# One image pair per DMA, with stores issued two pairs late, in a rotation kernel

## The chip, the cores and the metric

The kernel runs on one core of one Trainium2 chip. The metric is the device time of one execution in microseconds (us); the time quoted for a kernel is the median of several executions. A profile is a hardware trace of one further execution. In it PE is the matrix engine, ACT the scalar engine, DVE the vector engine, POOL the GpSimd engine, and SP the engine that issues the loads. "SPq" and "ACTq" are those engines' instruction queues where they issue DMAs.

## The reference

The input `x` has 32 x 3 = 96 images of 256 x 256 float32 values (25.17 MB), and so has the output. Each image is turned by 90 degrees:

```
batch, c, h, w = 32, 3, 256, 256
return np.rot90(x, k=1, axes=(-2, -1)).astype(np.float32)
```

No arithmetic is done on the values: 25.17 MB are read, moved to other places and 25.17 MB are written.

## The kernel before, in words

The 96 images are taken as 48 pairs. In SBUF a pair fills all 128 partitions: 64 partitions for each image, each holding four neighbouring rows (4 KB, one contiguous piece of DRAM). The pairs are grouped: eleven groups of four pairs (8 images, 2 MB), one of two pairs (1 MB) and two of one pair (512 KB each).

A group is loaded by one DMA on the SP queue (line 68) into a tile `S4` of `in_pool`, which has four buffers. Then each pair of the group goes through four steps:

- PE transposes it in eight pieces of 128x128 float32 into PSUM, tile `p1pair` (line 88);
- ACT casts each image's half to bf16 in two copies, tiles `bt` (line 96);
- PE multiplies by two exchange matrices, which reverse the order of rows, in four products into PSUM, tile `psum2` (line 102);
- DVE copies the result in two copies into the group's output tile `U4` (line 111).

When all the pairs of a group are done, one DMA on the ACT queue stores the group (line 118). `out_pool` has three buffers of 2 MB. The last three groups have tiles of their own (`tail_pool`), and their stores are issued after all compute (line 125).

PE, ACT and DVE each take their instructions in the order that the tile framework's scheduler writes; it puts transposes of the next pair between the products of the current one. The framework also adds the waits: a load waits until the transposes that read its buffer are done, a copy into `U4` waits until the store that read that buffer has landed, a store waits for its copies. DMAs get one of eight completion semaphores (`DMAHW0` to `DMAHW7`) in turn, loads and stores together in scheduled order, and a DMA is not issued before the previous DMA on its semaphore has landed. Instructions behind a waiting DMA on the same engine wait too.

In the trace the tile `S4` appears as `S_91`, `S_175` and so on, one name for each group, and `U4` as `U_93`, `U_177`, ..., `U_tail_1083`.

Of the kernel before, what the change touches and what calls it, by code (L numbers as in the profile page):

```python
# [1 line left out]

# [5 lines left out]


@with_exitstack
def kernel(
    ctx: ExitStack,
    tc: tile.TileContext,
    x: bass.AP,
    out: bass.AP,
):
    nc = tc.nc
    B, C, H, W = x.shape
    assert H == W == 256  # L20
    P = 128
    N = B * C

    x_v4 = x.rearrange("b c (p d) w -> (b c) p d w", d=4)
    out_v4 = out.rearrange("b c (p d) w -> (b c) p d w", d=4)

    GROUPS = [8] * 11 + [4, 2, 2]
    assert sum(GROUPS) == N
    assert all(g % 2 == 0 for g in GROUPS)

    fp32 = mybir.dt.float32
    bf16 = mybir.dt.bfloat16

    const_pool = ctx.enter_context(tc.tile_pool(name="const", bufs=1))
    in_pool = ctx.enter_context(tc.tile_pool(name="in_pool", bufs=4))
    bt_pool = ctx.enter_context(tc.tile_pool(name="bt_pool", bufs=4))
    out_pool = ctx.enter_context(tc.tile_pool(name="out_pool", bufs=3))
    tail_pool = ctx.enter_context(tc.tile_pool(name="tail", bufs=1))
    psum1_pool = ctx.enter_context(tc.tile_pool(name="psum1", bufs=2, space=bass.MemoryType.PSUM))
    psum2_pool = ctx.enter_context(tc.tile_pool(name="psum2", bufs=2, space=bass.MemoryType.PSUM))  # L40

    identity = const_pool.tile([P, P], fp32)
    make_identity(nc, identity)

    exchh = []
    for hh in range(2):
        e = const_pool.tile([P, P // 2], bf16, name=f"exch{hh}")
        nc.gpsimd.memset(e, 0.0)
        nc.gpsimd.affine_select(
            out=e,  # L50
            in_=e,
            compare_op=mybir.AluOpType.not_equal,
            fill=1.0,
            base=-(P - 1) + hh,
            pattern=[[2, P // 2]],
            channel_multiplier=1,
        )
        exchh.append(e)

    TAIL_N = 3  # L60
    deferred_stores = []

    i0 = 0
    for gi, G in enumerate(GROUPS):
        is_tail = gi >= len(GROUPS) - TAIL_N
        G2 = G // 2
        S4 = in_pool.tile([P, G2, 4, W], fp32, tag="S", name="S4")
        nc.sync.dma_start(
            out=S4[:],
            in_=x_v4[i0 : i0 + G].rearrange("(j q) p d w -> (q p) j d w", q=2),  # L70
        )
        S4_r = S4.rearrange("pp j d (k par) -> pp j d k par", par=2)

        if is_tail:
            U4 = tail_pool.tile(
                [P, G2, 4, W], fp32, tag=f"tail{gi}", name=f"U4_tail{gi}"
            )
        else:
            U4 = out_pool.tile([P, G2, 4, W], fp32, tag="U", name="U4")

        for j in range(G2):
            p1pair = psum1_pool.tile([P, 2, 2, W], fp32, name="p1pair")
            p1pair_r = p1pair.rearrange(
                "k dd q (pt dquad) -> k dd q pt dquad", dquad=4
            )
            for d4 in range(4):
                for par in range(2):
                    nc.tensor.transpose(  # L88
                        p1pair_r[:, 1 - par, :, :, d4],
                        S4_r[:, j, d4, :, par],  # L90
                        identity,
                    )
            bts = []
            for q in range(2):
                bt = bt_pool.tile([P, 2, W], bf16, name="bt")
                nc.scalar.copy(out=bt[:], in_=p1pair[:, :, q, :])  # L96
                bts.append(bt)

            psum2 = psum2_pool.tile([P, 2, 2, W], fp32, name="psum2")
            for hh in range(2):  # L100
                for q in range(2):
                    nc.tensor.matmul(  # L102
                        out=psum2[64 * q : 64 * q + 64, hh],
                        lhsT=exchh[hh][:],
                        rhs=bts[q][:],
                        start=True,
                        stop=True,
                    )

            for hh in range(2):  # L110
                nc.vector.tensor_copy(  # L111
                    out=U4[:, j, 2 * hh : 2 * hh + 2, :], in_=psum2[:, hh]
                )

        if is_tail:
            deferred_stores.append((i0, G, U4))
        else:
            nc.scalar.dma_start(
                out=out_v4[i0 : i0 + G].rearrange("(j q) p d w -> (q p) j d w", q=2),
                in_=U4[:],  # L120
            )
        i0 += G

    for s0, G, U4 in deferred_stores:
        nc.scalar.dma_start(
            out=out_v4[s0 : s0 + G].rearrange("(j q) p d w -> (q p) j d w", q=2),
            in_=U4[:],
        )


# [1 line left out]
_INS = ['x']  # L132
_OUTS = [((32, 3, 256, 256), 'float32')]


# [23 lines left out]
```

## Time and profile before

| | |
|---|---|
| median of 6 runs | 128.02 us (127.48 to 128.65) |
| profiled execution | 128.3 us, of which the span from the first to the last instruction is 126.5 us |
| PE busy | 103.4 us (82%), 576 matmuls |
| DVE busy | 60.6 us (48%), 96 copies |
| ACT busy | 51.9 us (41%), 96 casts and a table load |
| DMA | 50.42 MB in 12742 packets, mean 398 GB/s |
| DMAs issued by the kernel | 14 loads on SP, 14 stores on ACT |

"Busy" for an engine is the time in which it runs instructions; DMA issues are not counted. The DMA share is the mean busy share of the core's 16 DMA engines and can read slightly over 1, as packets overlap. "To landing" is the time from a DMA's issue to its completion semaphore. q1 is the queue of the loads and q10 that of the stores; both run on the same 16 DMA engines.

### The profile page before, as it was taken

Reading aid. Unit: us, or ns where it says so; the run is one execution under the profiler, and the core shown is the slowest. Engines: PE = TensorE matmul, PEld = TensorE weight load, DVE = VectorE, ACT = ScalarE, POOL = GpSimd, SP = SyncE. Lnnn points to the kernel's source line nnn. Section 1 sums busy time; section 2 is a strip of 40 time slices with the busy share of each in tenths; the row PEclk is TensorE's granted clock in tenths of the full one; section 3 lists DMA queues with packets and bytes.
Section 4 is the critical chain, followed back from the end, with each engine's and each line's share of the span. In section 5 each row is a group of like instructions: output and inputs, shape, how many; then the busy total and the mean of one; then the engine's idle time right before and its main releaser. Section 6 shows DMA issues by size and latency. Waiting matters only on the chain.

```text
span 126.5 us, 1521 instructions
## 1 busy us (share of the span) xinstructions
PE 103.4 (82%) x576; PEld 64.1 (51%) x576; DVE 60.6 (48%) x96; ACT 51.9 (41%) x97; POOL 1.2 (1%) x10
## 2 busy tenths in 40 slices
PE   0019999999999999999995995799999599999600
PEld 0018366565576566655752753476555456655300
DVE  0000447484566646745643741904940954746530
ACT  4003353445633563456336336053465065436300
POOL 3000000000000000000000000000000000000000
PEclk9999999999999999999999999689999999999965
DMA  3999999999999999999999999999999999999993
GB/s 85 399 370 409 417 416 409 412 378 413 426 418 423 421 418 425 414 417 425 418 421 426 417 425 416 418 414 427 416 421 426 416 416 426 414 376 394 405 411 140
DMA packets 12742, 50.42 MB, mean 398 GB/s; under 512 B 448, under 2 KB 448, under 8 KB 12736
## 3 DMA queue, kind: packets, MB, share of 16 engines
q1 hardware_dynamic: 6368, 25.17, 49.7%
q10 hardware_dynamic: 6368, 25.17, 48.7%
q8 instruction: 4, 0.07, 0.2%
q14 instruction: 2, 0.02, 0.0%
HBM read 25.17 MB, written 25.17 MB: 398 GB/s over the span
## 4 chain that ended last, share of the span: by engine, by line
DMA 41%; PE 40%; DVE 7%; ACT 6%; issue 1%; DVEq 1%; ACTq 0%
PE p1pair L88 25%; DMA out_dram<-U_597 18%; DMA out_dram<-U_345 16%; DMA S_91<-in_x_dram 6%; ACT bt L96 6%; DVE U_597 L111 2%; DVE U_849 L111 1%; DVE U_345 L111 1%; DVE U_tail_1017 L111 1%; DVE U_tail_1060 L111 1%; PE psum_127 L102 1%; PE psum_107 L102 1%; PE psum_419 L102 1%; PE psum_671 L102 1%; PE psum_1007 L102 1%
## 5 line engine op out<-in xcount | busy, mean ns | idle before, releaser
L96 ACT CAST bt<-p1pair 128x512 bf16<-128x512 f32 x96 | 50.6, 593 | 66.7 <-PE p1pair L88 66.7
L102 PEld LDWEIGHTS <-exch_81 128*64 128x64 bf16 x96 | 8.6, 108 | 19.2 <-issue 3.9
L88 PE MATMUL p1pair<-identity,S_91 128*128 128x128 f32 x32 | 6.9, 374 | 9.0 <-DMA S_91<-in_x_dram 9.0
L88 PEld LDWEIGHTS p1pair<-identity,S_91 128*128 128x128 f32 x32 | 5.5, 216 | 10.9 <-issue 10.9
L102 PEld LDWEIGHTS <-exch_86 128*64 128x64 bf16 x96 | 6.0, 110 | 5.1 <-issue 5.0
L111 DVE COPY U_93<-psum_107 128x512 f32<-128x512 f32 x2 | 1.3, 686 | 13.7 <-PE psum_107 L102 13.7
L88 PE MATMUL p1pair<-identity,S_679 128*128 128x128 f32 x32 | 6.1, 332 | 0.0
L88 PEld LDWEIGHTS p1pair<-identity,S_679 128*128 128x128 f32 x32 | 4.8, 212 | 2.1 <-issue 1.7
L88 PE MATMUL p1pair<-identity,S_175 128*128 128x128 f32 x32 | 5.7, 306 | 0.0
L88 PE MATMUL p1pair<-identity,S_763 128*128 128x128 f32 x32 | 5.6, 310 | 0.0
L88 PEld LDWEIGHTS p1pair<-identity,S_175 128*128 128x128 f32 x32 | 4.4, 208 | 2.4 <-issue 1.6
L88 PEld LDWEIGHTS p1pair<-identity,S_763 128*128 128x128 f32 x32 | 4.6, 210 | 1.7 <-issue 1.3
L88 PE MATMUL p1pair<-identity,S_847 128*128 128x128 f32 x32 | 5.3, 300 | 0.0
L88 PE MATMUL p1pair<-identity,S_343 128*128 128x128 f32 x32 | 5.3, 299 | 0.0
L88 PE MATMUL p1pair<-identity,S_931 128*128 128x128 f32 x32 | 5.3, 299 | 0.0
L88 PE MATMUL p1pair<-identity,S_427 128*128 128x128 f32 x32 | 5.3, 299 | 0.0
L88 PE MATMUL p1pair<-identity,S_595 128*128 128x128 f32 x32 | 5.3, 299 | 0.0
L88 PE MATMUL p1pair<-identity,S_511 128*128 128x128 f32 x32 | 5.3, 299 | 0.0
L88 PE MATMUL p1pair<-identity,S_259 128*128 128x128 f32 x32 | 5.3, 299 | 0.0
L88 PEld LDWEIGHTS p1pair<-identity,S_847 128*128 128x128 f32 x32 | 4.3, 209 | 1.7 <-issue 1.3
L88 PEld LDWEIGHTS p1pair<-identity,S_595 128*128 128x128 f32 x32 | 4.3, 208 | 1.7 <-issue 1.3
L88 PEld LDWEIGHTS p1pair<-identity,S_343 128*128 128x128 f32 x32 | 4.3, 208 | 1.7 <-issue 1.3
(164 smaller groups left out, 154.8 us busy)
## 6 DMA issues: line engine op xcount, KB each, us to landing
S_91<-in_x_dram SPq DMA_DIRECT2D x1, 2048.0 KB, 8.2
S_175<-in_x_dram SPq DMA_DIRECT2D x1, 2048.0 KB, 13.4
S_259<-in_x_dram SPq DMA_DIRECT2D x1, 2048.0 KB, 17.9
S_343<-in_x_dram SPq DMA_DIRECT2D x1, 2048.0 KB, 22.5
S_427<-in_x_dram SPq DMA_DIRECT2D x1, 2048.0 KB, 15.3
out_dram<-U_93 ACTq DMA_DIRECT2D x1, 2048.0 KB, 15.6
S_511<-in_x_dram SPq DMA_DIRECT2D x1, 2048.0 KB, 15.6
out_dram<-U_177 ACTq DMA_DIRECT2D x1, 2048.0 KB, 17.0
```

The costliest lines, as they stand in the source:

```text
L88: nc.tensor.transpose(p1pair_r[:, 1 - par, :, :, d4], S4_r[:, j, d4, :, par], identity,)
L96: nc.scalar.copy(out=bt[:], in_=p1pair[:, :, q, :])
L102: nc.tensor.matmul(out=psum2[64 * q : 64 * q + 64, hh], lhsT=exchh[hh][:], rhs=bts[q][:], start=True, stop=True,)
L111: nc.vector.tensor_copy(out=U4[:, j, 2 * hh : 2 * hh + 2, :], in_=psum2[:, hh])
```

## The change

Groups are given up. Each of the 48 pairs has its own 512 KB load, its own output tile and its own 512 KB store. `in_pool` has eight buffers of 512 KB (4 MB; before, four of 2 MB) and `out_pool` ten of 512 KB (5 MB; before, three of 2 MB, and 2 MB of tail tiles). The store of a pair is not issued right after its copies, but two pairs later, on the ACT queue between that later pair's transposes and its casts; after the last pair the remaining two are issued. The compute of a pair is the same.

```
-    GROUPS = [8] * 11 + [4, 2, 2]
-    in_pool = ctx.enter_context(tc.tile_pool(name="in_pool", bufs=4))
+    in_pool = ctx.enter_context(tc.tile_pool(name="in_pool", bufs=8))
-    out_pool = ctx.enter_context(tc.tile_pool(name="out_pool", bufs=3))
-    tail_pool = ctx.enter_context(tc.tile_pool(name="tail", bufs=1))
+    out_pool = ctx.enter_context(tc.tile_pool(name="out_pool", bufs=10))
...
+    STORE_LAG = 2
+    pending = []
+    def flush_store():
+        s0, U4s = pending.pop(0)
+        nc.scalar.dma_start(
+            out=out_v4[s0 : s0 + 2].rearrange("q p d w -> (q p) d w"),
+            in_=U4s[:],
+        )
+    for pi in range(NPAIR):
+        i0 = 2 * pi
+        S4 = in_pool.tile([P, 4, W], fp32, tag="S", name="S4")
         nc.sync.dma_start(
             out=S4[:],
-            in_=x_v4[i0 : i0 + G].rearrange("(j q) p d w -> (q p) j d w", q=2),
+            in_=x_v4[i0 : i0 + 2].rearrange("q p d w -> (q p) d w"),
         )
...
+        U4 = out_pool.tile([P, 4, W], fp32, tag="U", name="U4")
...
+        if len(pending) >= STORE_LAG:
+            flush_store()
...
+        pending.append((i0, U4))
-        if is_tail:
-            deferred_stores.append((i0, G, U4))
-        else:
-            nc.scalar.dma_start(
-                out=out_v4[i0 : i0 + G].rearrange("(j q) p d w -> (q p) j d w", q=2),
-                in_=U4[:],
-            )
-    for s0, G, U4 in deferred_stores:
-        nc.scalar.dma_start(...)
+    while pending:
+        flush_store()
```

In the built program of the changed kernel the order on the engines is this. PE runs the eight transposes of pair i+1 and then the four products of pair i, pair after pair. ACT runs the store of pair i-2 and then the two casts of pair i. The first eight loads take the semaphores 0 to 7; after a mixed stretch the loads settle on the semaphores 0, 2, 4 and 6 and the stores on 1, 3, 5 and 7. After the last load the remaining stores (pairs 38 to 47) take all eight in turn.

More of the change, by code (lines that the diff above doesn't have):

```diff
@@ L22 @@
     N = B * C
+    NPAIR = N // 2
     x_v4 = x.rearrange("b c (p d) w -> (b c) p d w", d=4)
     out_v4 = out.rearrange("b c (p d) w -> (b c) p d w", d=4)
-    GROUPS = [8] * 11 + [4, 2, 2]
-    assert sum(GROUPS) == N
-    assert all(g % 2 == 0 for g in GROUPS)
     fp32 = mybir.dt.float32
@@ L58 @@
         exchh.append(e)
[L60 to L67, printed above, removed]
+    STORE_LAG = 2
[9 more added lines that the diff above has]
+        S4 = in_pool.tile([P, 4, W], fp32, tag="S", name="S4")
@@ L68 @@
         nc.sync.dma_start(
             out=S4[:],
-            in_=x_v4[i0 : i0 + G].rearrange("(j q) p d w -> (q p) j d w", q=2),
+            in_=x_v4[i0 : i0 + 2].rearrange("q p d w -> (q p) d w"),
         )
-        S4_r = S4.rearrange("pp j d (k par) -> pp j d k par", par=2)
-        if is_tail:
-            U4 = tail_pool.tile(
-                [P, G2, 4, W], fp32, tag=f"tail{gi}", name=f"U4_tail{gi}"
-            )
-        else:
-            U4 = out_pool.tile([P, G2, 4, W], fp32, tag="U", name="U4")
@@ L81 @@
[L81 to L84, printed above, removed]
-            )
[L86 to L113, printed above, removed]
@@ L115 @@
-        if is_tail:
-            deferred_stores.append((i0, G, U4))
-        else:
-            nc.scalar.dma_start(
-                out=out_v4[i0 : i0 + G].rearrange("(j q) p d w -> (q p) j d w", q=2),
-                in_=U4[:],
-            )
-        i0 += G
-    for s0, G, U4 in deferred_stores:
[L125 to L128, printed above, removed]
+        S4_r = S4.rearrange("pp d (k par) -> pp d k par", par=2)
@@ new lines @@
+        U4 = out_pool.tile([P, 4, W], fp32, tag="U", name="U4")
+        p1pair = psum1_pool.tile([P, 2, 2, W], fp32, name="p1pair")
+        p1pair_r = p1pair.rearrange("k dd q (pt dquad) -> k dd q pt dquad", dquad=4)
+        for d4 in range(4):
+            for par in range(2):
+                nc.tensor.transpose(
+                    p1pair_r[:, 1 - par, :, :, d4],
+                    S4_r[:, d4, :, par],
+                    identity,
+                )
+        if len(pending) >= STORE_LAG:
+            flush_store()
@@ new lines @@
+        bts = []
+        for q in range(2):
+            bt = bt_pool.tile([P, 2, W], bf16, name="bt")
+            nc.scalar.copy(out=bt[:], in_=p1pair[:, :, q, :])
+            bts.append(bt)
+        psum2 = psum2_pool.tile([P, 2, 2, W], fp32, name="psum2")
+        for hh in range(2):
+            for q in range(2):
+                nc.tensor.matmul(
+                    out=psum2[64 * q : 64 * q + 64, hh],
+                    lhsT=exchh[hh][:],
+                    rhs=bts[q][:],
+                    start=True,
+                    stop=True,
+                )
@@ L132 @@
+        for hh in range(2):
+            nc.vector.tensor_copy(
+                out=U4[:, 2 * hh : 2 * hh + 2, :], in_=psum2[:, hh]
+            )
+        pending.append((i0, U4))
+    while pending:
+        flush_store()
 _INS = ['x']
```

## The prediction

> **What bounds the kernel now.** I read first the page's busy shares beside its DMA rows, then the load queue's waits and issue times, then the transfers by window, and last the time line of the end.
>
> ```profile
> span 126.5 us, 1521 instructions
> PE 103.4 (82%) x576; PEld 64.1 (51%) x576; DVE 60.6 (48%) x96; ACT 51.9 (41%) x97; POOL 1.2 (1%) x10
> DMA  3999999999999999999999999999999999999993
> ...
> HBM read 25.17 MB, written 25.17 MB: 398 GB/s over the span
> ```
>
> No engine is full, and the DMA engines are, in every slice but the first and the last.
>
> ```profile
> 4.00:24.00 20.00, 14.94 (x73) 9.56 (x73) 5.90 (x10) 6.44 (x12) 0.00 (x0) 1.00 1.02 405
> 24.00:28.00 4.00, 3.71 (x23) 2.28 (x23) 3.06 (x5) 1.12 (x3) 0.00 (x0) 1.00 1.02 383
> 28.00:68.00 40.00, 39.44 (x227) 24.18 (x226) 21.47 (x35) 20.59 (x40) 0.00 (x0) 1.00 1.02 420
> 68.00:112.00 44.00, 38.31 (x219) 24.16 (x219) 23.95 (x39) 18.89 (x37) 0.00 (x0) 0.96 1.02 420
> 112.00:116.00 4.00, 4.00 (x25) 2.42 (x25) 2.41 (x4) 2.10 (x5) 0.00 (x0) 1.00 0.89 363
> 116.00:124.00 8.00, 3.02 (x17) 1.50 (x15) 3.77 (x6) 1.44 (x3) 0.00 (x0) 0.81 1.03 411
> ```
>
> The last columns of these windows are clock, DMA share and GB/s: 405 with loads alone, 420 with both queues, 411 with stores alone. There is little to win inside: 24:28 and 112:116 miss 0.35 and 0.54 us against 420.
>
> ```profile
> 27.89 0.37 SPq L68 DMA_DIRECT2D S_511<-in_x_dram  x1
> 36.34 0.37 SPq L68 DMA_DIRECT2D S_595<-in_x_dram  x1
> 44.80 0.37 SPq L68 DMA_DIRECT2D S_679<-in_x_dram  x1
> ...
> 118.59 0.35 ACTq L125 DMA_DIRECT2D out_dram<-U_tail_1060  x1
> 120.01 1.29 DVE L111 COPY U_tail_1083<-psum_1097 128x512 f32<-128x512 f32 x2 [1.46 <-PE psum_1097 L102]
> 121.33 0.35 ACTq L125 DMA_DIRECT2D out_dram<-U_tail_1083  x1
> ```
>
> The loads leave as PE frees buffers, 8.46 us apart for four pairs: compute's own pace is 2.115 us a pair, while the DMA needs 1.05 MB / 420 = 2.50 us. So compute runs ahead until the output buffers stop it (a DVE copy waited 3.8, 3.2 and 3.1 us for a store). At the end the last store is issued at 121.33 and lands after 4.1, at 125.4; the span ends 1.1 later, and 1.8 of the profiled 128.3 us lie outside the span.
>
> **The change part by part.** The sum is an absolute time of the last landing, set against 125.4.
>
> Head. The first load is 0.52 MB, not 2.10. By the windows, 0.59 MB had moved by 4.0 us and 2.21 by 8.0, so 2.10 by 7.7; the load landed at 8.9 (0.74 + 8.16), 1.2 later. The small one lands at 3.8 + 1.2 = 5.0 and PE starts 4 us sooner. I cost this at nothing: the load queue keeps the DMA full either way. Without that cover it would be worth -4.
>
> Issues. 34 more loads on SP at 0.37 are 12.6 us on an engine that only waits. 34 more stores on ACT at 0.38 are 12.9 us; ACT's pair is then 2 x 0.535 + 0.38 = 1.45 us, under PE's 2.115. Nothing, and up to 13 us if ACT were the bound. PE and DVE keep their instructions; PE's order loses the mixing of transposes and products. In the new order pair i's casts need pair i-2's store issued, which needs its copies (1.29 after its products); casts end 1.29 + 0.38 + 1.07 = 2.8 us after those products and are used 1.22 + 2.115 = 3.3 us after them. Cover 0.5 us a pair; gone, up to 0.5 x 10 pairs = 5 at the end, where nothing else hides it.
>
> Completion packets. 16 small ones a DMA: 448 now, 1536 after, 68 DMAs more. From below: windows 48:64 with 48 of them still run at 420, cost 0. From above: 118:124 also has 48, for three times fewer bytes, at 410 instead of 420: 6 us x 2.4% / 3 DMAs = 0.05 us each, 3.3 in all. Both queues being busy for most of the kernel is nearer to the first: 0.01 each, 0.6 by the end of the loads.
>
> The speed of 512 KB DMAs themselves: the two last stores land at 118.59 + 5.6 = 124.2 and at 125.4, 1.2 us apart for 0.52 MB, some 430 GB/s behind a backlog. The Trainium skill says otherwise: "DMA: Bandwidth & Descriptors", section "Rules for kernel authors", asks for at least 1 MiB a DMA for maximum bandwidth, and its table of measured bandwidth has 341 GB/s at 1 MB; 50.33 MB at that rate would take 148 us, an estimate from that page. The row disagrees wherever a queue holds several DMAs, so the sum goes by the row.
>
> The semaphores. This is the part that decides. Eight DMAs in all are in flight at most, about four a queue, and a store waits in ACT's order for the DMA before it on its semaphore, with the casts behind it and PE behind those. In mid-kernel a store waits for the fourth store before it, four in flight hold 4 x 2.5 = 10 us of work, and the DMA never runs dry: cost 0. But the store of pair 38 (U_1000) has semaphore 6, whose last user is the load of pair 44 (S_1142). Compute cannot pass that landing, and ten stores are then left. When does load 44 land?
> - First store: now 13.74 + 1.29 = 15.0, 6.0 after PE's start at 9.04. After: 5.0 + 6.0 = 11.0. Its data follow 1.1 us later (first load: issued 0.74, moving just before 2.0) to 3.9 (first store: issued 22.78, nothing on its queue at 25.5 to 26.5); I take 2.0: 13.0. Loads moved by then: 0.59 + 9.0 x 0.405 = 4.24 MB, 8 loads (7.4 to 9.5).
> - From there the queues share evenly (841 and 842 packets at 48:64). The first stores come at 2.1 us and the store of pair 4 waits for load 10, so loads gain 1 to 2 more: 9.5 ahead (8 to 11).
> - Load 44 is wholly moved with 45 loads and 35.5 stores, 42.2 MB: 13.0 + 37.96 / 0.420 = 103.4, with packets 104.0, with landing (1.2 for one queue, more for two) 105.5.
>
> The end from there. Issue 0.38 and casts of pair 40 1.07: 1.5. PE has six pairs of transposes (1.22 each) and eight of products (2.115 - 1.22 = 0.89): 14.4. Copies 1.29 with handovers 1.35. The last store: 1.24 to move, 1.1 and 1.2 to start and land, 3.5 in all, or 4.1 as now: 3.7. Sum 21.0, so 105.5 + 21.0 = 126.5, **1.1 us after** the 125.4 of now. The DMA alone would be quicker: 50.33 - 42.2 = 8.1 MB from 104.0 at 0.411 move by 123.8. So the end of the new kernel is compute, with the DMA idle between stores. 128.3 + 1.1 = 129.4 for the profiled execution, which stands 0.3 above the median: **129.1 us**.
>
> **The rivals.**
> A, the DMA stays full to the end, as now. For it: the backlog at the end holds it full now. Against: 2.115 us a pair from compute against 1.25 a store. It lands at 123.8 + 1.2 = 125.0, or 124.4 if the packets cost nothing: 127.6 to 127.0, say 127.3. It needs 1.5 us less of compute after load 44's landing (21.0 against 19.5), one pair done earlier than the semaphore allows.
>
> B, slower by PE's clock: the ACT wait at the store of pair 38 lasts long enough for PE's clock to drop as it did once.
>
> ```profile
> 68.00:70.00 2.00, 0.34 (x5) 0.14 (x4) 1.66 (x3) 0.36 (x1) 0.00 (x0) 1.00 1.03 424
> ...
> 78.00:80.00 2.00, 0.00 (x0) 0.00 (x0) 1.33 (x3) 0.12 (x1) 0.00 (x0) 0.99 1.02 422
> 80.00:82.00 2.00, 1.99 (x9) 1.18 (x10) 2.00 (x4) 0.00 (x0) 0.00 (x0) 0.50 1.02 418
> 82.00:84.00 2.00, 2.00 (x12) 1.83 (x10) 0.40 (x1) 0.92 (x2) 0.00 (x0) 0.66 1.01 410
> ```
>
> PE idle for 1.7 us at 68 kept its clock; 2 us at 78 halved it for 3.4 us, which costs 1.7 us of a PE-bound end. Store 34 would free compute 1.3 us before load 44 lands when loads are 9.5 ahead; with the usual 0.4 of waiting PE idles 1.7, just under. At 8 ahead it idles 5.4 (two stores of 2.5 between) and load 44 lands 1.9 later: 129.1 + 1.9 + 1.7 = 132.7; at 9, 129.1 + 0.6 + 1.7 = 131.4. It decides from an idle of 2 us, below some 9.3.
>
> C, small DMAs run slower, at the upper price of the packets: 129.1 + 2.7 = 131.8. Against it is the 1.2 us between the last two landings.
>
> D, nothing changes: the gain of 0.9 in the two dips (24:28, 112:116) and the loss at the end cancel, 128.0 to 128.4. That would be my sum with 10.3 loads ahead, as each load is 1.25 us.
>
> **How the numbers follow.** A measurement here cannot tell less than about 0.5%, 0.64 us: 127.4 to 128.7 is "same". My sum has 0.42 (128.4 to 130.0, of it 0.11 below 128.7), A 0.20 (0.13 of it below 127.4, the middle being 127.3), B 0.28, C 0.05, D 0.05. Faster: 0.13. Same: 0.07 + 0.11 + 0.05 = 0.23, raised to 0.25, as D's cancelling has more ways than I priced. Slower: the rest, 0.62. Likeliest is my sum, 129.1, with its own range 128.4 to 130.0. The whole range runs from 127.1, just above the lowest A, to 131.8, which takes in C and the nearer half of B; 0.04 of A and 0.12 of B are left out.
>
> **What the new profile would show.** The store of pair 38 as the longest wait of ACT's queue, ending with the landing of S_1142 near 105; DMA at 420 GB/s in mid-kernel (C: 400 or less); DMA share down to some 0.7 in the last 12 us, with PE full to about 121 (A: DMA share at 1 there); the clock column at 1.00 after 105 (B: 0.50 for 3 us). PE starts near 5 us and the first store is issued near 11. I am wrong if compute's pace in the new order isn't 2.115, if loads share the DMA unevenly with stores (each load more ahead moves the end 1.25 us earlier, until A), or if four DMAs a queue don't keep it full.

## The result, and the profile after

| | kernel before | changed kernel |
|---|---|---|
| median, measured side by side | 127.82 us (127.41 to 128.98, 20 runs) | 128.80 us (128.55 to 129.65, 10 runs) |
| ratio to before | 1 | **1.0074**, 95% interval 1.0047 to 1.0101 |
| profiled execution, its span | 128.3 us, 126.5 us | 128.57 us, 126.8 us |

The changed kernel is slower by 0.7%, about 1 us. Measured once more beside the kernel before, on another chip (below), it was slower by 0.3%. The two intervals overlap from 1.0047 to 1.0057, so "half a per cent slower" is the best short statement, and causes of a few tenths of a microsecond are near what can be told apart here. The ratio is estimated over the executions of both kernels and is not the quotient of the two medians, from which it differs by up to 0.25% in the tables here.

The page of the changed kernel, busy shares and DMA rows:

```profile
span 126.8 us, 1718 instructions
PE 98.7 (78%) x576; PEld 64.5 (51%) x576; DVE 61.9 (49%) x96; ACT 52.7 (42%) x97; POOL 1.3 (1%) x10
DMA  4999999999999999999999999999999999999992
...
HBM read 25.17 MB, written 25.17 MB: 397 GB/s over the span
```

The DMA engines are still the full resource, 397 GB/s against 398. The transfers by the same windows as in the prediction; the last three columns are clock, DMA share and GB/s:

```profile
4.00:24.00 20.00, 15.05 (x88) 10.94 (x89) 7.73 (x12) 6.83 (x13) 0.00 (x0) 1.00 1.00 384
24.00:28.00 4.00, 3.80 (x16) 2.00 (x15) 1.29 (x2) 2.00 (x5) 0.00 (x0) 0.57 1.02 416
28.00:68.00 40.00, 34.86 (x210) 22.80 (x209) 22.36 (x35) 17.96 (x34) 0.00 (x0) 1.00 1.03 419
68.00:112.00 44.00, 37.22 (x216) 23.85 (x215) 22.95 (x37) 19.47 (x37) 0.00 (x0) 1.00 1.03 419
112.00:116.00 4.00, 4.00 (x30) 2.92 (x30) 3.07 (x6) 2.63 (x6) 0.00 (x0) 1.00 1.02 414
116.00:124.00 8.00, 3.76 (x24) 1.96 (x23) 4.47 (x8) 2.50 (x5) 0.00 (x0) 0.95 1.00 409
```

Mid-kernel moves 419 GB/s where it moved 420. The two old dips are filled (24 to 28 us: 416 for 383; 112 to 116 us: 414 for 363), and what that wins is about what is lost at the start, 384 for 405 between 4 and 24 us. The end, from 116 us, moves 409 for 411. Taken over the first 122 us, the kernel before and then the changed one:

```profile
0.00:122.00 122.00, 103.42 (x576) 64.11 (x576) 60.57 (x96) 51.88 (x97) 1.25 (x10) 0.98 1.00 405
0.00:122.00 122.00, 98.69 (x576) 64.48 (x576) 61.88 (x96) 52.67 (x97) 1.25 (x10) 0.99 1.01 406
```

So in these two profiles the changed kernel has moved as many bytes by 122 us as the kernel before, and its later end comes from what follows.

The time line of ACT around the forecast hold; `U_976` is the store of pair 37, `U_1000` of pair 38, `U_1216` of the last pair, and the bracket is ACT's idle time before a line and what ended it:

```profile
102.75 0.34 ACTq L61 DMA_DIRECT2D out_dram<-U_976  x1
103.18 1.07 ACT L93 CAST bt<-p1pair 128x512 bf16<-128x512 f32 x2 [1.38 <-DMA out_dram<-U_880]
106.11 0.34 ACTq L61 DMA_DIRECT2D out_dram<-U_1000  x1
106.54 0.59 ACT L93 CAST bt<-p1pair 128x512 bf16<-128x512 f32 x1 [2.29 <-DVE U_1024 L108]
106.64 0.35 ACTq L61 DMA_DIRECT2D out_dram<-U_1024  x1
107.02 1.57 ACT L93 CAST bt<-p1pair 128x512 bf16<-128x512 f32 x3
...
118.35 0.34 ACTq L61 DMA_DIRECT2D out_dram<-U_1168  x1
...
120.15 0.34 ACTq L61 DMA_DIRECT2D out_dram<-U_1192  x1
121.86 0.34 ACTq L61 DMA_DIRECT2D out_dram<-U_1216  x1
```

In mid-kernel a store leaves ACT every 2.5 us. Pair 38's comes 3.36 us after pair 37's. The bracket names a copy by DVE, but a store isn't held by the copies of the pair after it, and its own had long ended: of the waits of that moment the profile names the one that came last. The load with the same semaphore (`S_1142`, pair 44) was issued at 96.11 and took 9.9 us to land: 106.0. From 109.6 on the remaining pairs run on compute's pace, a store issued every 1.7 to 1.8 us, and the last store is issued 15.75 us after pair 38's and lands 4.1 later, at 126.0; in the kernel before it was 125.4. But the stores don't land at compute's pace. Their times from issue to landing (last column) fall one by one:

```profile
out_dram<-U_1168 ACTq DMA_DIRECT2D x1, 512.0 KB, 5.1
out_dram<-U_1192 ACTq DMA_DIRECT2D x1, 512.0 KB, 4.5
out_dram<-U_1216 ACTq DMA_DIRECT2D x1, 512.0 KB, 4.1
```

Added to the issue times these are landings at 123.5, 124.7 and 126.0, some 1.25 us apart, which is the time that 0.52 MB take at 420 GB/s. In this execution the DMA has a backlog up to the last store, so compute alone does not set the end.

A DMA ends with one small completion packet from each of the 16 DMA engines. For the last store they come at 124.5 us on average in both profiles; the last of the 16 comes at 125.1 in the kernel before and at 125.5 in the changed one. These 0.3 us are as much as the two profiled executions differ by.

### The profile page after: what moved, and what is told of

It reads as the page before. It is cut to its first block, busy times and chain, and to the rows that moved or that the text cites. A ratio compares the mean times of both kernels' runs of the same rounds, so it can differ in the third digit from the quotient of the medians.

```text
span 126.8 us, 1718 instructions
## 1 busy us (share of the span) xinstructions
PE 98.7 (78%) x576; PEld 64.5 (51%) x576; DVE 61.9 (49%) x96; ACT 52.7 (42%) x97; POOL 1.3 (1%) x10
## 4 chain that ended last, share of the span: by engine, by line
DMA 67%; PE 21%; ACT 2%; issue 2%; DVE 2%; ACTq 1%; DVEq 0%
PE p1pair L81 13%; DMA S_326<-in_x_dram 10%; DMA out_dram<-U_496 8%; DMA out_dram<-U_880 8%; DMA out_dram<-U_784 8%; DMA out_dram<-U_592 8%; DMA out_dram<-U_688 8%; DMA out_dram<-U_400 8%; DMA out_dram<-U_304 7%; DMA S_88<-in_x_dram 2%; ACT bt L93 2%; PE psum_247 L99 1%; ACTq L61 1%; PE psum_127 L99 1%; DVE U_1024 L108 1%
## 5 line engine op out<-in xcount | busy, mean ns | idle before, releaser
L93 ACT CAST bt<-p1pair 128x512 bf16<-128x512 f32 x96 | 51.4, 589 | 66.5 <-PE p1pair L81 9.2
L99 PEld LDWEIGHTS <-exch_78 128*64 128x64 bf16 x96 | 8.5, 107 | 19.9 <-issue 14.1
L99 PEld LDWEIGHTS <-exch_83 128*64 128x64 bf16 x96 | 5.3, 107 | 12.1 <-issue 12.0
L108 DVE COPY U_90<-psum_104 128x512 f32<-128x512 f32 x2 | 1.3, 687 | 8.1 <-PE psum_104 L99 8.1
L81 PE MATMUL p1pair<-identity,S_88 128*128 128x128 f32 x8 | 2.0, 423 | 4.0 <-DMA S_88<-in_x_dram 4.0
L99 PE MATMUL psum_247<-bt,exch_78 128*64 128x512 bf16 x2 | 1.1, 586 | 3.7 <-ACT bt L93 3.7
L108 DVE COPY U_232<-psum_247 128x512 f32<-128x512 f32 x2 | 1.3, 686 | 5.1 <-PE psum_247 L99 5.1
L81 PEld LDWEIGHTS p1pair<-identity,S_88 128*128 128x128 f32 x8 | 1.6, 221 | 4.0 <-issue 4.0
L108 DVE COPY U_208<-psum_223 128x512 f32<-128x512 f32 x2 | 1.3, 686 | 2.2 <-PE psum_223 L99 2.2
L108 DVE COPY U_1048<-psum_1063 128x512 f32<-128x512 f32 x2 | 1.3, 686 | 2.1 <-PE psum_1063 L99 2.1
L108 DVE COPY U_568<-psum_583 128x512 f32<-128x512 f32 x2 | 1.3, 687 | 1.7 <-PE psum_583 L99 1.7
L108 DVE COPY U_448<-psum_463 128x512 f32<-128x512 f32 x2 | 1.3, 687 | 1.6 <-PE psum_463 L99 1.6
L81 PEld LDWEIGHTS p1pair<-identity,S_278 128*128 128x128 f32 x8 | 1.6, 221 | 0.8 <-issue 0.8
L81 PE MATMUL p1pair<-identity,S_278 128*128 128x128 f32 x8 | 2.0, 427 | 0.0
L108 DVE COPY U_400<-psum_415 128x512 f32<-128x512 f32 x2 | 1.3, 687 | 1.4 <-PE psum_415 L99 1.4
L108 DVE COPY U_952<-psum_967 128x512 f32<-128x512 f32 x2 | 1.3, 687 | 1.4 <-PE psum_967 L99 1.4
L108 DVE COPY U_856<-psum_871 128x512 f32<-128x512 f32 x2 | 1.3, 686 | 1.3 <-PE psum_871 L99 1.3
L108 DVE COPY U_904<-psum_919 128x512 f32<-128x512 f32 x2 | 1.3, 687 | 1.3 <-PE psum_919 L99 1.3
L108 DVE COPY U_1000<-psum_1015 128x512 f32<-128x512 f32 x2 | 1.3, 686 | 1.3 <-PE psum_1015 L99 1.3
L108 DVE COPY U_688<-psum_703 128x512 f32<-128x512 f32 x2 | 1.3, 686 | 1.2 <-PE psum_703 L99 1.2
L108 DVE COPY U_808<-psum_823 128x512 f32<-128x512 f32 x2 | 1.3, 687 | 1.2 <-PE psum_823 L99 1.2
L108 DVE COPY U_760<-psum_775 128x512 f32<-128x512 f32 x2 | 1.3, 687 | 1.2 <-PE psum_775 L99 1.2
```

Source lines behind the costliest of these rows:

```text
L81: nc.tensor.transpose(p1pair_r[:, 1 - par, :, :, d4], S4_r[:, d4, :, par], identity,)
L99: nc.tensor.matmul(out=psum2[64 * q : 64 * q + 64, hh], lhsT=exchh[hh][:], rhs=bts[q][:], start=True, stop=True,)
L108: nc.vector.tensor_copy(out=U4[:, 2 * hh : 2 * hh + 2, :], in_=psum2[:, hh])
```

## The experiments

Ratios are to the kernel before on the same chip, with their 95% intervals. The table is in the order of the ratio; the sections follow the order of the questions.

| kernel | median, us | before there, us | ratio |
|---|---|---|---|
| DMAs alone, 2 MB | 127.29 | 128.31 | 0.9928 (0.9903 to 0.9953) |
| DMAs alone, 512 KB | 127.19 | 128.31 | 0.9929 (0.9900 to 0.9958) |
| DMAs alone, 512 KB, one queue | 127.30 | 128.17 | 0.9957 (0.9923 to 0.9992) |
| groups of before, store one group late | 127.78 | 128.17 | 0.9973 (0.9947 to 0.9999) |
| changed, less compute in the tail | 128.44 | 128.46 | 0.9987 (0.9964 to 1.0010) |
| changed, six input buffers | 128.46 | 128.46 | 1.0006 (0.9979 to 1.0032) |
| changed, hold taken off ACT | 128.53 | 128.17 | 1.0027 (0.9999 to 1.0056) |
| changed kernel again | 128.69 | 128.46 | 1.0030 (1.0004 to 1.0057) |
| 1 MB DMAs, store one group late | 128.98 | 128.17 | 1.0044 (1.0013 to 1.0075) |
| changed, twelve input buffers | 129.24 | 128.46 | 1.0069 (1.0035 to 1.0102) |
| changed, tail stores on SP | 129.47 | 128.31 | 1.0106 (1.0073 to 1.0139) |
| changed, no lag | 138.23 | 128.31 | 1.0779 (1.0747 to 1.0811) |

### Are 512 KB DMAs slower than 2 MB ones?

```
-    in_pool = ... bufs=8
+    in_pool = ... bufs=16
...                                  (transposes, casts, products and copies removed)
-        pending.append((i0, U4))
+        pending.append((i0, S4))
+        flush_store()
```

The other kernel does the same to the kernel before: groups of 2 MB, stores sent from the input tiles.

> The changed kernel's 48 loads and 48 stores of 512 KB alone: the compute is left out, each pair is stored as it was loaded, so the output is not turned. Theory 1: 50.33 MB at 420 GB/s are 119.8 us, with a start of 1.9, an end of 1.2 and 3 us around it 125 to 126.5 us, within 0.6 us of the run with 2 MB DMAs. Theory 2: at least 1 us above the run with 2 MB DMAs, with a lower rate in mid-kernel.

> The kernel before's 14 loads and 14 stores (2 MB, at the end 1 MB and twice 512 KB) alone: the compute is left out, each group is stored as it was loaded, so the output is not turned. Theory 1: 125 to 126.5 us, as with 512 KB. Theory 2: at least 1 us below the run with 512 KB DMAs.

Windows of the 512 KB kernel, clock, DMA share and GB/s last:

```profile
4.00:14.00 10.00, 0.00 (x0) 1.00 0.96 350
14.00:122.00 108.00, 0.00 (x0) 1.00 1.03 420
```

and of the 2 MB kernel:

```profile
4.00:14.00 10.00, 0.00 (x0) 1.00 0.99 371
14.00:122.00 108.00, 0.00 (x0) 1.00 1.03 422
```

127.19 and 127.29 us, both above the 125 to 126.5 us expected but alike: the size costs no time that can be measured as long as several DMAs are queued (420 against 422 GB/s over 108 us is 0.5 us). That ends rival C. The Trainium skill's page "DMA: Bandwidth & Descriptors", section "Rules for kernel authors", asks for 1 MiB or more a DMA; these two runs don't show the loss that the page's table, measured with DMAs issued from GpSimd, gives for smaller ones. The second thing these runs give is a floor for these two orders of DMAs: without any compute they are only 0.7% faster than the kernel before. Another order could lie lower, since between 4 and 14 us these two move 350 and 371 GB/s, which loses 1.7 and 1.2 us of DMA time.

### Is it the lag, or the pairs?

First the pairs without the lag:

```
-        if len(pending) >= STORE_LAG:
-            flush_store()
...
         pending.append((i0, U4))
+        flush_store()
```

> The changed kernel without its lag: each pair's store is written right after its copies, one part of the change undone. In the built order ACT then runs the casts of two pairs and two stores in turn, the store of pair 39 waits for the load of pair 44, and PE's order mixes transposes with products as before the change. Theory 1: the same hold at the end, but compute at the slower 2.115 us a pair of that order instead of 1.75, eight pairs: 128.8 + 2.9 = 131.7 us (130.5 to 132.5). Theory 2: the lag has no part in it, 128.8 within 0.5.

7.8% slower, more than expected. ACT's time line shows why: four casts, then two stores that wait for their copies, then four casts again.

```profile
59.67 2.05 ACT L90 CAST bt<-p1pair 128x512 bf16<-128x512 f32 x4 [3.21 <-PE p1pair L81]
62.74 2.09 ACTq L61 DMA_DIRECT2D out_dram<-U  x2
64.93 2.05 ACT L90 CAST bt<-p1pair 128x512 bf16<-128x512 f32 x4 [3.21 <-PE p1pair L81]
```

Two pairs take 64.93 - 59.67 = 5.26 us, 2.63 a pair, longer than the 2.50 that the DMA needs, so compute is the bound; 48 pairs lose 6 us by that. The DMA lives on the loads that are ahead, 416 GB/s from 68 to 84 us and 402 up to 112, and then has only what compute hands it, 228 GB/s. With stores of one pair, the lag is what makes the change bearable at all: a store that waits for its copies right behind them stops the casts of the next pair. The edit also brought back the mixed order of transposes and products on PE. In the kernel before that order took 2.115 us a pair, which is under the DMA's 2.50, so the order alone doesn't explain the 2.63.

Then the other half, the groups with the lag:

```
-    out_pool = ... bufs=3
-    tail_pool = ...
+    out_pool = ... bufs=4
...
+            if j == 0 and len(pending) >= 1:     # after the transposes of the next group's first pair
+                flush_store()
...
-            nc.scalar.dma_start(out=..., in_=U4[:])
+        pending.append((i0, G, U4))
```

> The kernel before with its 2 MB groups, and of the change the lagged store alone: every group's store is issued by ACT one group later, after the first transposes of the next group are written, from a pool of four output tiles; the separate tail tiles go. Splitting the two parts of the change: if the loss of the changed kernel comes from the pairs (more DMAs, more completions on shared semaphores, the early start of the second queue), this one stays at the kernel before, 0.997 to 1.001. If it comes from the lag, that is from stores that start later and so leave more bytes for the end, this one is slower: the first store moves by one group of four pairs (near 8 us) and the DMA has only loads for that time, which at the 405 GB/s of loads alone against 420 mixed costs about 0.3 us, and the last group's stores come together after the last copies, for 1.002 to 1.010.

The better half of the expectation came: 0.9973. Its waits of DVE and a window of its end:

```profile
DVE U L113 <- DMA out_dram<-U: 2.5, 1, 2.5
```

```profile
118.00:122.00 4.00, 0.00 (x0) 0.00 (x0) 0.00 (x0) 0.00 (x0) 0.00 (x0) 0.50 1.03 421
```

The kernel before had three such waits (3.8, 3.2 and 3.1 us). Here compute ends earlier: the last store is issued at 116.39 instead of 121.33, and from 118 to 122 us the DMA moves 421 GB/s for 409. The run does not tell the late store from the fourth output buffer that came with it, but the lag as such is not what loses time. This is the fastest kernel of the study that does the whole work; its interval only just leaves 1 out.

Between the two, 1 MB DMAs:

```
-    GROUPS = [8] * 11 + [4, 2, 2]
+    GROUPS = [4] * 22 + [2] * 4
-    out_pool = ... bufs=4
+    out_pool = ... bufs=6
```

> Between the two kernels: DMAs of 1 MB (two pairs) for 22 groups and then of 512 KB for four, four input tiles, six output tiles, and each store one group late. With 1 MB the semaphores that eight DMAs share are met half as often as in the changed kernel, and the end still has small stores. If the hold at the shared semaphore is what costs the changed kernel its 0.5 to 1 us, this has none of it or one placed elsewhere, and lies at 0.995 to 1.000 of the kernel before (the DMAs alone with no compute gave 0.993, which is the floor for it). If the loss is in the lag or in the early second queue, it lies with the changed kernel, 1.003 to 1.008.

1.0044, so it did not beat the kernel before. But its loss has a place of its own, which the expectation hadn't seen. Two windows:

```profile
14.00:16.00 2.00, 2.00 (x11) 1.11 (x10) 0.90 (x2) 1.23 (x3) 0.00 (x0) 1.00 1.04 270
16.00:18.00 2.00, 2.00 (x12) 1.12 (x11) 1.06 (x3) 1.07 (x2) 0.00 (x0) 1.00 0.61 193
```

Four input tiles of 1 MB are half the input buffering of before. The fifth load landed at 15.9 us, the sixth was issued only at 14.55, when a tile came free, and the first store (14.63) was as late: the DMA had little to move and lost (420 - 270 + 420 - 193) x 2 / 420 = 1.8 us. So this run says nothing on the shared semaphores.

### What does the hold at pair 38 cost?

The changed kernel run again, unedited, so that the next runs have it on their own chip:

> The changed kernel itself, once more, beside the next three on the same chip: 1.005 to 1.010 of the kernel before, as at first.

It came out below that range, 1.0030. Its profile shows the hold by name, and longer than the first time:

```profile
101.89 0.34 ACTq L61 DMA_DIRECT2D out_dram<-U  x1
102.32 1.07 ACT L93 CAST bt<-p1pair 128x512 bf16<-128x512 f32 x2 [1.45 <-DMA out_dram<-U]
106.40 0.34 ACTq L61 DMA_DIRECT2D out_dram<-U  x1
106.84 0.58 ACT L93 CAST bt<-p1pair 128x512 bf16<-128x512 f32 x1 [3.44 <-DMA S<-in_x_dram]
```

```profile
104.00:108.00 4.00, 1.60 (x12) 1.25 (x12) 1.29 (x2) 1.16 (x3) 0.00 (x0) 1.00 1.03 417
108.00:112.00 4.00, 4.00 (x18) 2.30 (x18) 1.63 (x3) 1.97 (x4) 0.00 (x0) 0.57 1.02 416
112.00:118.00 6.00, 6.00 (x44) 4.25 (x43) 4.64 (x8) 3.22 (x6) 0.00 (x0) 1.00 0.98 399
118.00:122.00 4.00, 3.17 (x20) 1.65 (x20) 2.75 (x5) 2.15 (x4) 0.00 (x0) 1.00 0.84 343
```

ACT waits 3.44 us for a load, PE is busy for 1.60 of 4 us, its clock falls to a mean of 0.57 for the next 4 us, and the DMA then runs at 343 GB/s from 118 to 122 us. That is the course of rival B. Here compute does set the end: the last store, issued at 123.5, finds no backlog (KB and us to landing last):

```profile
out_dram<-U ACTq DMA_DIRECT2D x1, 512.0 KB, 2.6
```

It lands 2.6 us later, at 126.1. The hold costs about (21 x 6 + 77 x 4) / 420 = 1.0 us of DMA time, against 0.1 us in the first profile, and yet the span is 127.0 against 126.8 us. The same kernel has a short and a long hold in different executions.

First attempt to take the hold away: the stores from pair 38 on go to SP.

```
-        nc.scalar.dma_start(
+        (nc.sync if s0 >= 2 * 38 else nc.scalar).dma_start(
```

> The changed kernel, with the stores of the last ten pairs (38 to 47) issued from SP's queue behind its last load, so that no cast on ACT stands behind a waiting store there. Theory 1 (the end is set by compute, which is held on ACT until the load of pair 44 lands and then has eight pairs left): compute goes on from about 100 us, the last copies are done before 119, the DMA is full to the end and the last landing comes 0.5 to 1.2 us earlier, 127.7 to 128.3 us. Theory 2 (512 KB DMAs move fewer bytes a second, and the end is only where the bytes run out): the DMA was full there already, 128.8 us within 0.3.

1.0106, the wrong direction. But the edit changed something else too. The copies of DVE in the tail:

```profile
108.75 1.29 DVE L108 COPY U<-psum 128x512 f32<-128x512 f32 x2 [1.48 <-PE psum L99]
110.74 1.29 DVE L108 COPY U<-psum 128x512 f32<-128x512 f32 x2 [0.70 <-PE psum L99]
113.27 1.29 DVE L108 COPY U<-psum 128x512 f32<-128x512 f32 x2 [1.24 <-PE psum L99]
115.26 1.29 DVE L108 COPY U<-psum 128x512 f32<-128x512 f32 x2 [0.70 <-PE psum L99]
```

They come 2.26 us apart on average (2.0 and 2.5 in turn) where the changed kernel does a pair in 1.75: with the stores gone from ACT's queue the scheduler wrote PE's instructions in another order, products split by transposes. The run is no test of the hold; what it shows is that PE's order is worth half a microsecond a pair once the tail is bound by compute.

Second attempt, with the order kept: the next pair's transposes are written ahead of this pair's casts, products and copies.

```
+    def back_end(i0, p1pair):            # casts, products, copies of one pair
...
+        if held is not None:
+            back_end(*held)
+        held = (i0, p1pair)
...
+        (nc.sync if s0 >= 2 * 38 else nc.scalar).dma_start(
```

> The changed kernel with two edits: the transposes of the next pair are written ahead of this pair's casts, products and copies, so that TensorE keeps each pair's eight transposes and four products together (the order it had in the changed kernel), and the stores from pair 38 on are issued by SP instead of ACT, so that no cast stands behind a store that waits for load 44. It mends the tail experiment of before, in which moving the stores had also split TensorE's order (2.26 us a pair). Theory 1 (the hold on ACT sets the end of the changed kernel): the casts run on past 101 us at the 1.75 us a pair of the changed kernel's tail or the DMA's pace, the last packets fall near 125, and the time is 0.3 to 0.8 us under the changed kernel, a ratio of 0.997 to 1.001 to the kernel before. Theory 3 (the hold is covered, because the DMA is nearly full until 122 us in any case): no change from the changed kernel, 1.003 to 1.007.

ACT's time line and the end's window:

```profile
102.97 2.05 ACT L74 CAST bt<-p1pair 128x512 bf16<-128x512 f32 x4 [1.47 <-DMA out_dram<-U]
105.94 1.07 ACT L74 CAST bt<-p1pair 128x512 bf16<-128x512 f32 x2 [0.91 <-PE p1pair L109]
107.64 1.07 ACT L74 CAST bt<-p1pair 128x512 bf16<-128x512 f32 x2 [0.64 <-PE p1pair L109]
```

```profile
118.00:122.00 4.00, 0.00 (x0) 0.00 (x0) 1.22 (x2) 0.00 (x0) 0.00 (x0) 0.92 1.02 419
```

The hold on ACT is gone, though the stores themselves still wait on SP (pair 38's is issued at 106.38): casts run every 1.7 us from 103 us, PE is done by 118, and the DMA is full to 122 us. The time is 1.0027, which lies in the ranges of neither theory clearly: against the changed kernel's second measurement (1.0030) nothing is won, against the first result (1.0074) 0.5%. The completion packets of the last store show what became of the gain. They come at 123.9 us on average here and at 124.5 in the first profile of the changed kernel, 0.6 earlier; but the last of the 16 comes at 125.5 in both.

Three more edits of the changed kernel, each with its tail placed differently. Less compute in the tail (for pairs 40 to 47 casts and products are left out):

```
+        if pi < 40:
...
+        else:
+            for hh in range(2):
+                nc.vector.tensor_copy(out=U4[:, 2 * hh : 2 * hh + 2, :], in_=p1pair[:, hh])
```

> The changed kernel, with the casts and the products left out for the last eight pairs (40 to 47): their transposes are copied straight to the output tile, so the output of these pairs is not right. The DMAs, their semaphores and the hold of pair 38's store stay. Theory 1 (after the hold compute sets the end): a pair then costs 1.3 us of DVE instead of 1.75 of PE, the stores come as fast as the DMA takes them, and the end comes 0.6 to 1.3 us earlier than the changed kernel's. Theory 3 (the DMA's own course, its head above all, makes the loss): no change, within 0.3 us.

and twelve or six input buffers (`in_pool` with `bufs=12` or `bufs=6`), which move loads further ahead or less far:

> The changed kernel with twelve load buffers instead of eight. In the built program it is then the store of pair 34, not 38, that waits for the load of pair 44. Theory 1: compute is held from about 96 us until that load lands (some 101 to 105, as the loads have the DMA to themselves meanwhile), and has twelve pairs of 1.75 us left: 1.5 to 4 us later than the changed kernel. Theory 3: more buffers do no harm, within 0.3 us.

> The changed kernel with six load buffers instead of eight. In the built program the store of pair 40 waits for the load of pair 44, and pair 39's store for pair 35's as in mid-kernel; compute has two pairs fewer left at the hold. Theory 1: 0.4 to 1.0 us earlier than the changed kernel, about as the kernel before. Theory 3: no change, within 0.3 us.

By the medians the light tail is 0.25 us under the changed kernel and six buffers 0.23 us under it (by the ratios 0.4% and 0.2%, 0.5 and 0.3 us). Neither reaches the least gain that theory 1 allowed, 0.6 and 0.4 us, and by the medians both lie in the 0.3 us of theory 3. Twelve buffers are 0.55 us over it, which is neither "within 0.3" nor the 1.5 us or more of theory 1: compute then passes the hold 5 us earlier (pair 34's store at 101.27 us) with four more pairs left. So what the hold costs in time is not shown to be more than a few tenths of a microsecond. Their windows from 118 to 122 us, in that order:

```profile
118.00:122.00 4.00, 0.00 (x0) 0.00 (x0) 0.00 (x0) 0.00 (x0) 0.00 (x0) 0.50 1.04 424
```

```profile
118.00:122.00 4.00, 0.97 (x4) 0.22 (x3) 2.37 (x4) 0.51 (x2) 0.00 (x0) 0.83 1.02 416
```

```profile
118.00:122.00 4.00, 3.35 (x23) 2.04 (x22) 3.07 (x6) 2.64 (x6) 0.00 (x0) 1.00 0.83 335
```

Set beside the ratios, the column GB/s seems to sort the variants: 424, 416 and 419 (hold off ACT) go with 0.9987, 1.0006 and 1.0027; 343 (changed, again), 335 (twelve) and 338 (tail stores on SP) with 1.0030, 1.0069 and 1.0106; only the first profile of the changed kernel, with 418 and 1.0074, doesn't fit. But a ratio comes from six to twelve executions and a window from one. Beside the time of the same execution the order is gone: 424 goes with 128.94 us, 416 with 128.40, 419 with 128.56 and 418 with 128.57; 343 goes with 128.74, 335 with 129.27 and 338 with 128.53. That what compute leaves idle on the DMA near the end is paid for in full is therefore not shown. In five of these seven profiles the last store lands between 125.8 and 126.1 us, whether the DMA was full before or not; the others are less compute (126.3) and twelve buffers (126.7).

### Where does the fall in rate at the start come from?

All kernels with 512 KB DMAs show less than 420 GB/s somewhere in the first 19 us. My guess, after the first runs, was the start of the second queue. The test has all DMAs on SP's queue, without compute:

```
     def flush_store():
         s0, U4s = pending.pop(0)
-        nc.scalar.dma_start(
+        nc.sync.dma_start(
...
+        if len(pending) > 6:
+            flush_store()
```

> The kernel of DMAs alone in 512 KB (transposes, products, casts and copies are left out, the stores send what lies in the input tiles), with the stores issued by SP on the loads' own queue, six pairs behind the loads. It tests the fall in rate near 4 to 14 us (350 GB/s with two queues, whether compute was there or not). If the start of the second queue makes the fall, 4 to 14 us shows 400 GB/s or more here, and the time is 126.0 to 127.0 us against 127.2 with two queues. If the first stores make it whatever queue they are on, the fall is there again and the time is the same or, with one queue of its own order, up to 1 us more.

```profile
4.00:14.00 10.00, 0.00 (x0) 1.00 0.98 358
14.00:122.00 108.00, 0.00 (x0) 1.00 1.03 420
```

The fall is there with one queue (358 GB/s; 350 with two), and the time is not better, as the expectation had it for the case that the first stores make the fall on whatever queue. The guess is wrong. The first stores are a part of it, but the cause stays open. For them: windows of 1 us show the fall two to five microseconds after the first store's issue in the changed kernel run again (issued at 10.27; 311, 287 and 340 GB/s from 12 to 15 us) and in the 2 MB DMAs alone (issued at 9.02; 299 and 287 from 11 to 13 us), so it isn't a matter of 512 KB either; and the groups with the lag, whose first store is issued at 22.5 us, have 408 GB/s from 4 to 14 us. Against them: the same groups show no fall behind their first store (401 GB/s or more in each microsecond from 22 to 28 us), and in the first profile of the changed kernel the rate is at 303 and 258 GB/s from 4 to 6 us, ahead of the first store at 9.40.

## Why the prediction was right, and where its steps were not

The time was right (129.1 forecast, 128.8 measured; ratio 1.0084 forecast, 1.0074 measured), and so was the sign. The hold at pair 38's store is what the profile shows, where and when the forecast put it. The step behind it, an end bound by compute "with the DMA idle between stores", is not what the first profile shows: the DMA is full to 122 us and the last stores land at its pace, 1.25 us apart. The second profile does show it (343 GB/s; the last store lands after 2.6 us instead of 4.1), with a last landing only 0.2 us later. That the forecast's number came out although the first profile took another way to it is luck. That the hold accounts for the difference is not shown either: the three runs that weaken, move or remove it (less compute in the tail, six buffers, hold off ACT) have ratios 0.0 to 0.4% below the changed kernel's second measurement, which itself lay 0.3% above the kernel before. What makes the changed kernel slower stays open; the profiles show that it isn't the bytes moved by 122 us.

- **Head, cost nothing.** Right in sum, with a detail missed. PE starts at 4.02 us (5.0 forecast), the first store is issued at 9.40 (11.0). Not foreseen was the fall to 349 GB/s from 4 to 14 us (398 before). It is paid back by an earlier first load (205 against 147 GB/s up to 4 us) and a better stretch from 14 to 28 us (418 against 404): by 28 us 10.16 MB had moved, before 10.22, 0.14 us of work.
- **Issues, cost nothing.** Right: 0.34 us each, and in mid-kernel ACT waits 1.4 us a pair for the fourth store before, so it has room.
- **"PE's order loses the mixing", up to 5 us.** The sign was wrong, and with it the pace: the forecast named a pace other than 2.115 as a sign of being wrong, and that came. Kept apart, eight transposes (1.15 us) and four products (0.55 to 0.65) take 1.70 to 1.80 a pair against the 2.115 of the mixed order. The feared gap for casts did not open. (The forecast's 1.29 + 0.38 + 1.07 is 2.74, not 2.8, and the cover 0.6.)
- **Completion packets, 0.6 us.** About right: 419 against 420 GB/s from 28 to 112 us is 0.2 us, and the kernels of DMAs alone, 420 against 422 GB/s from 14 to 122 us, differ by 0.5 us.
- **512 KB DMAs as fast as 2 MB ones.** Right, by the two kernels of DMAs alone.
- **The semaphore of pair 38.** Right in place and time: load 44 landed at 106.0 (105.5 forecast). Pair 4's store did wait for load 10, until 23.13 us with ACT idle for 4.89, and that was hidden, as said: the DMA moved 418 GB/s from 14 to 28 us. This wait, and not the one of pair 38 (2.29 us), was the longest of ACT for a DMA, against the forecast's sign.
- **21.0 us from there to the last landing.** Mis-sized: 20.0 (106.0 to 126.0). PE's 14.4 were 13.3, from the first product at 107.18 to the end of the last at 120.52, because of the faster order; casts took less, as the first products need only one of them; the landing took 4.1 and not 3.7, because of the backlog; behind an idle DMA it took 2.6. The last landing came 0.5 us after that of before instead of 1.1, and the profiled execution was 0.3 us longer instead of 1.1. The median came out near the forecast all the same, since it lies 0.2 above the profiled execution here and 0.3 below it before: on that last step the forecast was lucky.
- **"DMA share down to some 0.7 in the last 12 us".** Wrong for the first profile (1.02 from 112 to 122 us), nearer in the second (0.84 from 118 to 122). The first profile has rival A's picture, a DMA that stays full, and the second the forecast's, an end set by compute; their last landings are 0.2 us apart. A's time, 127.3 us, did not come.
- **Rival B**, which the forecast set apart by an idle time of 2 us, happens in some executions: in the first profile PE idles 1.13 us in the hold and the clock reads 1.00, in the second it idles 2.28 us and the clock reads 0.57 from 108 to 112 us. It was priced at 2.3 us or more over the forecast; the execution that shows it is 0.2 us longer in span than the one that doesn't. That the rest of the loss is hidden under the DMA's backlog is argued, not shown. The boundary of 2 us isn't sharp: with twelve buffers an idle time of 1.55 us that ended at 67.10 was followed by a clock of 0.50 from 68 to 70 us, while 1.66 us in the kernel before (to 69.69) was not. (The idle time that the forecast read as 2 us from windows is 2.22, from 77.79 to 80.01.)

## What to carry to other kernels

Where the DMA engines are nearly full from end to end, as here, the size of a DMA and the order of the work matter little as long as they stay full; measure the DMAs alone first, since their time (0.7% less here) says about how much there is to win. A store issued from an engine that also computes stops that engine's work for whatever the store waits for, be it its own copies (7.8% over the kernel before without the lag) or an unrelated DMA on the same completion semaphore (2.3 to 3.4 us of ACT at pair 38, of which the time shows a few tenths at most); issue it late, and look for the shared semaphore where loads and stores stop alternating. A window of one profile belongs to the time of that execution: compare it with that, before setting it beside the median of others. An edit that moves a DMA to another queue can change the order of instructions on engines that it doesn't touch, so compare that order before reading the time as the effect of the edit.

## What the runs showed of the hardware that was not expected

- One DMA queue moves as much as two: 420 GB/s with loads and stores in one queue or in two, from 14 to 122 us.
- The 16 DMA engines don't end together. In kernels whose DMA is full to the end, the completion packets of the last store spread over 0.7 to 2.6 us (124.4 to 125.1 in the kernel before, 123.1 to 125.5 with the hold off ACT, 122.9 to 124.6 with groups and the lag, 123.3 to 124.7 for 512 KB DMAs alone), and in kernels whose end is bound by compute over 0.2 us (125.6 to 125.8, changed kernel again). So what the hold off ACT won for the average DMA engine was not won for the slowest. Why some engines lag is open.
- A stretch of PE idleness in the hold halved its clock for some 3.4 us in one execution (PE busy 1.60 of 4 us, then a mean clock of 0.57 over 4 us) and not in another (2.65 of 4 us, clock 1.00).
- The fall in rate in the first 14 us doesn't need compute, nor a second queue (350 and 358 GB/s without compute), nor DMAs of 512 KB (371 GB/s with 2 MB); its cause wasn't found.
